# Moving the second stream's shifted inputs ahead of its low-rank products, and the first stream's v inputs and the whole second prelude behind the making of k's operands

## The chip, the core and the metric

The kernel runs on one core of one Trainium2 chip. TensorE (PE) multiplies matrices, with a sequencer of its own for weight loads (PEld); VectorE (DVE) and ScalarE (ACT) do elementwise work; GpSimd (POOL) does a few memsets; SyncE (SP) issues every DMA, one after the other, from one queue. Each engine has its own list of instructions; the trace shows the lists run in the order of the program, and an engine that waits at one instruction holds up the rest of its list. The metric is device microseconds of one execution.

## The reference

Two request groups ("streams" 0 and 1, 512 tokens by 1024 features each) pass through the same two layers. Layer 0 is an RWKV-7 time mixing with a forward and a backward scan, layer 1 a two-dimensional neighbourhood attention. The change touches the inputs of layer 0 only:

```
xn = rms_norm(x, pre_norm_g[0])
x_prev = jnp.pad(xn[:, :-1], ((0, 0), (1, 0), (0, 0)))
x_next = jnp.pad(xn[:, 1:], ((0, 0), (0, 1), (0, 0)))
xx = 0.5 * (x_prev + x_next) - xn
lerp = lambda j: xn + xx * mu[j]
r, k, v = heads(lerp(0) @ w_r), heads(lerp(1) @ w_k), heads(lerp(2) @ w_v)
z = xn @ w_z
for d in range(2):
    w_log = -softplus(-(w0[d] + tanh(lerp(3 + d) @ w1[d]) @ w2[d])) - 0.5
    a = sigmoid(a0[d] + (lerp(5 + d) @ a1[d]) @ a2[d])
    ...
```

`lerp(j)` is called a shifted input here; `lerp(3..6) @ w1, a1` are the low-rank products (1024 features to 4 times 64).

## The kernel before

Activations lie transposed: 128 features on the partitions and 512 tokens along the row, so a stream is 8 tiles of 128x512 (`k` = 0..7). Every fp32 product is split into a high and a low half of fp32r, and three products are made of one (hi·hi, hi·lo, lo·hi). A weight column (1024x128) comes in two DMAs `raw`; ACT casts each to `whi`, DVE subtracts to get `wlo` (four buffers of each). A column is 24 products of 128x512 on PE (lines 423 to 425 in the front, 802 to 804 in the scan stage). An operand pair (hi, lo) lies in two of 18 `act` buffers, nine pairs.

**The front** is all that comes before the scan stage. Its parts:

- prelude of stream 0: load x, norm (L434 to L465), `xn` (L525), `xx` (L532, L533), the low-rank weights (L479 to L487), the low-rank products (96 products, L549 to L551, into the banks `pf`, `pm`, `us`), their tail (L557 to L574), the shifted inputs for v (L581, 8 tiles, each saved to DRAM as `dlv`);
- eight columns z of stream 0, with its normalised x as operand;
- eight columns k of stream 0; the operands come from `shifted(0, 1)`: `xr` (L599) on DVE, cast on ACT, subtraction on DVE (L373 `act<-xr`). Each column's sums of squares go through L642, L646 and L649 to DRAM as `dss`. After the eighth they are loaded, rooted and inverted (L660, L662, L663) and stored as `drn`;
- prelude of stream 1: the same norm, `xn` and `xx`; then 8 pairs `ls` (ACT cast, DVE subtraction L373 `ls<-xn`) and the 96 low-rank products; the tail; then 24 shifted inputs for k, r and v (L581), each saved (`dlk`, `dlr`, `dlv`); `xn` is saved as `dlz`. All tiles `ls`, pairs and shifted inputs alike, share four buffers, taken in the order of the code;
- the operands of stream 0's r, `shifted(0, 0)`.

The tail of the low-rank products (L557 to L574) handles two pairs of results one after the other. For each pair: ACT copies `pf` (L562), DVE makes L563, L565, L570; then twice ACT L572 into the same 64 rows `u`, and a DMA saves them as `dhid`. There is one buffer `lm` and one buffer `lr`, and `u` is a part of `lr`: the second L572 waits until the first save has read `u`, and the second pair waits for the saves of the first.

**The scan stage** begins with columns r of stream 0 and the preparation of the first pair of heads: `rb` is loaded from `drn`, `k` from `dk`, `r` from `dr`; then L854 on DVE, L856 on ACT, L858 on DVE, the products L872 and L873 on PE, and from there the chain that feeds the scan's steps. Its order on PE, DVE and ACT is written by a planner that starts with all its clocks at zero, and so does not know when the front ends. L1622 are products without use that keep PE busy.

**The order in the front** is made by a scheduler that works through a simulated timeline: code that stands earlier has the higher priority, and an instruction is placed when its inputs are there in that simulated time. `run(g, (a, n))` advances generator `a` by `n` steps (yields) for each step of `g`; `both` joins two generators.

Of the kernel before, what the change touches and what calls it, by code (L numbers as in the profile page):

```python
# [14 lines left out]
ALU = mybir.AluOpType  # L15
# [214 lines left out]
class Trunk:  # L230
# [209 lines left out]
    def rstd(self, acc):  # L440
        run(self.rstds(acc))
        return acc
# [48 lines left out]
    def prelude(self, s):  # L491
        nc = self.nc
        vt, gps, act = nc.vector, nc.gpsimd, nc.scalar
# [3 lines left out]
        for k in range(KT):  # L497
            if s == 0 and k == self.WFIRST:
                self.first = [self.weight(self.a["w_z"][0])]
            t = self.t("xn", (P, T + 2), 16, F32, self.lp)  # L500
# [21 lines left out]
        xn, xx = [], []  # L522
        for k, t in enumerate(xs):
            x = t[:, 1:T + 1]
# [5 lines left out]
        for k, t in enumerate(xs):  # L530
# [3 lines left out]
            xx.append(u)  # L534
            yield
        self.shift[s] = xn, xx

        pm = self.p("pf", (P, 2, T))
        ps = (self.p("pm"), self.p("us"))
        for k in range(KT):  # L540
# [5 lines left out]
            for q2 in range(2):  # L546
                for out, w in ((pm[:, q2], self.wm), (ps[q2], self.wl)):
                    a, b = (m[:, k % 4] for m in w[2 * q2 + k // 4])
# [4 lines left out]
        for q2 in range(2):  # L553
# [21 lines left out]
                else:  # L575
                    self.save("hid", s, q, u)
            yield
        for kind, j in (("v", 2),) if s == 0 else (("k", 1), ("r", 0), ("v", 2)):
            for k in range(KT):
                t = self.t("ls", (P, T), 4, F32, self.lp)  # L580
                vt.scalar_tensor_tensor(t, xx[k], self.vec("mu", 8 * j + k), xn[k], op0=ALU.mult, op1=ALU.add)  # L581
                self.save("l" + kind, s, k, t)
                yield
        if s == 1:
# [550 lines left out]
    def step(self, q):  # L1135
# [59 lines left out]
        if both:  # L1195
            self.factors(q + 1, solved())
        else:
            run(solved())
# [513 lines left out]
    def run(self):  # L1712
        self.todo = [(s, pb) for s in range(2) for pb in range(4)]
        self.made, self.hid, self.shift = set(), {}, {}
        self.did = Counter()
        self.xz, self.os = [], [[], []]
        self.spare = None
        mid, prep, first = ExitStack(), ExitStack(), ExitStack()
        self.banks(mid, pf=1, pm=5 - self.SG - self.ZY, us=1)
        if self.SG:  # L1720
            self.banks(mid, pg=self.SG)
        self.zs = ExitStack()
        self.banks(self.zs, zy=self.ZY)
        self.gt = "zy"
        self.lp = self.pool(first, "right")
        a = self.prelude(0)
        for _ in range(self.FIRST):
            next(a)
        a = both(a, self.prelude(1))
        run(self.columns(0, "z", self.xz), (a, 1))  # L1730
        run(self.columns(0, "k", self.shifted(0, 1)), (a, 1))
        run(a)
        self.xr = self.shifted(0, 0)
        first.close()
        self.front = self.pool(mid, "right")
        self.pp = self.pool(prep, "right")
        self.AHEAD, self.AHEADW = self.SCAN_A, self.SCAN_W
        self.scan_phase(mid)
        self.rest(prep, mid)

    def rest(self, prep, mid):
# [15 lines left out]
        for p in range(self.NPA, NP):  # L1757
            run(self.inproj(0, self.xa, p), (a, self.POST0))
            queue.append(self.heads(0, p))
# [38 lines left out]
def both(*gs):  # L1798
    for g in gs:
        yield from g  # L1800
# [110 lines left out]
```

## Time and profile before

| | |
|---|---|
| median of three runs | 1686.07 us (1684.14 to 1687.42) |
| the profiled execution | 1683.88 us |
| its span, first to last instruction | 1682.1 us |
| what lies around the span | 1.8 us |
| PE busy / DVE busy / ACT busy | 1570.9 / 1227.8 / 984.0 us |
| mean granted TensorE clock | 0.971 |

The front takes roughly the first 190 us of the span: column z from 9 us, column k from 82 us, the last sum of squares of k at 170 us, the first instruction of the first pair of heads (L854) at 188.61 us. A row of the timeline gives the start in us, the duration in us, engine, line, operation, output and inputs, and in brackets the idle time of the engine just before and what ended it. A row of the windows gives for a stretch its length, then busy time and number of instructions of PE, PEld, DVE, ACT and POOL, the granted clock, the share of the DMA engines and GB/s. Busy times of successive instructions overlap a little, so a pace is read from one start to the next.

### The profile page before, as it was taken

What the parts mean: (1) busy time and instruction counts of PE and PEld (TensorE: products, weight loads), DVE (VectorE), ACT (ScalarE), POOL (GpSimd) and SP (SyncE); (2) the same over time, 40 slices, a digit from 0 to 9 for tenths busy, and PEclk for the clock granted to TensorE, in tenths of its full rate; (3) what the DMA queues carried; (4) which work ended last, traced back from release to release, by engine and by line L of the source; (5) the groups of instructions that cost most, each with busy time, mean ns of one, the idle gap of its engine ahead of it and who ended that gap; (6) DMA issues with size and microseconds to landing.
All of it is one profiled execution on the core that took longest, in us unless ns stands there. A gap on an engine that the chain in (4) does not pass through costs nothing.

```text
span 1682.1 us, 46291 instructions
## 1 busy us (share of the span) xinstructions
PE 1570.9 (93%) x18818; PEld 1201.2 (71%) x18818; DVE 1227.8 (73%) x2725; ACT 984.0 (58%) x1977; POOL 24.1 (1%) x94
## 2 busy tenths in 40 slices
PE   7989898899989998989998999999999899999998
PEld 6767666676766776767765767777777687777776
DVE  8985668688777697887888887865576856555564
ACT  5443655676655667755674665454577655555562
POOL 0000000000000000000000000000000000000000
PEclk9989999899999999999997999999999999999999
DMA  5435678678586786876776665554774347555553
GB/s 209 163 125 187 203 243 261 202 228 257 170 262 211 225 255 205 259 243 205 241 232 214 202 199 199 184 178 131 267 231 155 111 127 249 182 157 175 164 181 107
DMA packets 240821, 336.26 MB, mean 200 GB/s; under 512 B 53696, under 2 KB 119360, under 8 KB 240608
## 3 DMA queue, kind: packets, MB, share of 16 engines
q1 hardware_dynamic: 240608, 333.31, 61.6%
q8 instruction: 148, 2.42, 0.6%
q14 instruction: 65, 0.53, 0.1%
HBM read 227.71 MB, written 105.51 MB: 198 GB/s over the span
## 4 chain that ended last, share of the span: by engine, by line
PE 67%; DVE 11%; DMA 9%; ACT 8%; issue 4%; SPq 1%; DVEq 0%; POOL 0%; ACTq 0%; POOLq 0%
PE pm L802 7%; PE pg L423 6%; PE pg L424 6%; PE pg L425 6%; PE pm L804 5%; PE pm L803 5%; PE pf L1090 2%; PE sc L1433 2%; PE us L1209 2%; DMA cab<-dab 2%; PE po L1466 2%; PE pt L1451 2%; PE zy L1162 2%; PE us L1189 2%; PE zy L1213 1%
## 5 line engine op out<-in xcount | busy, mean ns | idle before, releaser
L802 PE MATMUL pm<-act,whi 128*128 128x512 f32 x640 | 287.6, 449 | 16.1 <-ACT act L771 7.2
L804 PE MATMUL pm<-act,wlo 128*128 128x512 f32 x640 | 256.7, 401 | 12.2 <-DVE wlo L723 12.2
L803 PE MATMUL pm<-act,whi 128*128 128x512 f32 x640 | 258.0, 403 | 5.1 <-DVE act L749 4.2
L423 PE MATMUL pg<-act,whi 128*128 128x512 f32 x448 | 182.4, 408 | 5.9 <-ACT act L372 5.5
L424 PE MATMUL pg<-act,whi 128*128 128x512 f32 x448 | 178.1, 398 | 0.1
L425 PE MATMUL pg<-act,wlo 128*128 128x512 f32 x448 | 177.5, 396 | 0.0
L802 PEld LDWEIGHTS pm<-act,whi 128*128 128x128 f32 x640 | 122.6, 192 | 63.8 <-issue 16.1
L372 ACT CAST whi<-raw 128x512 fp32r<-128x512 f32 x148 | 91.4, 619 | 129.3 <-PE pg L424 75.3
L804 PEld LDWEIGHTS pm<-act,wlo 128*128 128x128 f32 x640 | 123.4, 193 | 44.3 <-DVE wlo L723 16.9
L373 DVE TENSOR_TENSOR wlo<-raw,whi 128x512 fp32r<-128x512 f32 x148 | 101.4, 687 | 70.2 <-ACT whi L372 63.0
L803 PEld LDWEIGHTS pm<-act,whi 128*128 128x128 f32 x640 | 123.6, 193 | 29.6 <-DVE act L749 7.2
L723 DVE TENSOR_TENSOR wlo<-raw,whi 128x512 fp32r<-128x512 f32 x160 | 108.7, 684 | 42.9 <-ACT whi L721 39.5
L721 ACT CAST whi<-raw 128x512 fp32r<-128x512 f32 x160 | 98.1, 616 | 51.7 <-PE pm L803 14.5
L423 PEld LDWEIGHTS pg<-act,whi 128*128 128x128 f32 x448 | 84.8, 190 | 24.8 <-ACT act L372 6.1
L425 PEld LDWEIGHTS pg<-act,wlo 128*128 128x128 f32 x448 | 84.8, 189 | 17.9 <-issue 0.8
L424 PEld LDWEIGHTS pg<-act,whi 128*128 128x128 f32 x448 | 84.9, 190 | 17.4 <-issue 2.0
L996 DVE TENSOR_TENSOR N<-etmp,N 128x30 f32<-128x30 f32 (+14 forms) x240 | 78.5, 327 | 4.2
L994 DVE TENSOR_TENSOR etmp<-N 128x30 f32<-128x30 f32 (+14 forms) x240 | 78.3, 326 | 4.2
L1444 DVE CUSTOM_DVE_ANT_0 sb<-sc,bias 128x256 f32<-128x256 f32 x128 | 49.2, 419 | 31.1 <-PE pt L1451 23.5
L1090 PE MATMUL pf<-cab 64*64 64x128 f32 (+1 forms) x2048 | 67.9, 268 | 2.2 <-issue 2.1
L1447 ACT ACTIVATE sb<-sb,mx 128x256 f32<-128x256 f32 x128 | 63.9, 504 | 9.1 <-DVE mx L1446 9.0
L1113 DVE TENSOR_TENSOR AK<-zy,cc 128x256 f32<-128x256 f32 x63 | 26.6, 421 | 53.5 <-PE zy L1068 51.6
(389 smaller groups left out, 3389.7 us busy)
## 6 DMA issues: line engine op xcount, KB each, us to landing
dab<-ab SPq DMA_DIRECT2D x32, 1024.0 KB, 5.5
cab<-dab SPq DMA_DIRECT2D x64, 512.0 KB, 4.4
raw<-in_w_in_dram SPq DMA_DIRECT2D x128, 256.0 KB, 3.3
bias<-in_rpb_dram SPq DMA_DIRECT2D x32, 384.0 KB, 4.8
raw<-in_w_z_dram SPq DMA_DIRECT2D x32, 256.0 KB, 4.5
dz<-tmp SPq DMA_DIRECT2D x32, 256.0 KB, 3.0
raw<-in_w_k_dram SPq DMA_DIRECT2D x32, 256.0 KB, 4.0
dk<-tmp SPq DMA_DIRECT2D x32, 256.0 KB, 2.2
```

The lines of the kernel that those rows point to most:

```text
L372: self.nc.scalar.copy(hi, src)
L373: (eng or self.nc.vector).tensor_tensor(lo, src, hi.bitcast(F32), op=ALU.subtract)
L423: nc.tensor.matmul(ps, hi, x[k][0], start=(k == 0), stop=False)
L424: nc.tensor.matmul(ps, hi, x[k][1], start=False, stop=False)
L425: nc.tensor.matmul(ps, lo, x[k][0], start=False, stop=(k == KT - 1))
L721: nc.scalar.copy(hi, raw[h])
L723: nc.vector.tensor_tensor(lo, raw.pop(h), hi.bitcast(F32), op=ALU.subtract)
L802: nc.tensor.matmul(ps, hi[:, at], xh, start=(k == 0), stop=False)
L803: nc.tensor.matmul(ps, hi[:, at], xl, start=False, stop=False)
L804: nc.tensor.matmul(ps, lo[:, at], xh, start=False, stop=(k == KT - 1))
L996: vt.tensor_tensor(N[:, q + 1:, :q], tv, N[:, q + 1:, :q], op=ALU.add)
L1090: end = nc.tensor.matmul(st.f[half(a), h, 0, d, g] if st.last else st.f[half(a), h, :, d, g], ab[half(h), d, g, 2 * e[d] + 1 - a], rt if s ...
```

## The change

The 24 shifted inputs of stream 1 are made before its low-rank products instead of after them. The 8 shifted inputs for v of stream 0 leave its prelude and come after the whole prelude of stream 1. Prelude 0 is now run to its end before the code that makes the operands of k; prelude 1 starts after that code. The steps per column change from 1 to 0.6 (z) and 1.05 (k).

```diff
         self.shift[s] = xn, xx
+        if s == 1:
+            yield from self.shifts(1, (("k", 1), ("r", 0), ("v", 2)))
 
         pm = self.p("pf", (P, 2, T))
         ps = (self.p("pm"), self.p("us"))
...
-        for kind, j in (("v", 2),) if s == 0 else (("k", 1), ("r", 0), ("v", 2)):
+    def shifts(self, s, kinds):
+
+        xn, xx = self.shift[s]
+        for kind, j in kinds:
             for k in range(KT):
                 t = self.t("ls", (P, T), 4, F32, self.lp)
-                vt.scalar_tensor_tensor(t, xx[k], self.vec("mu", 8 * j + k), xn[k], op0=ALU.mult, op1=ALU.add)
+                self.nc.vector.scalar_tensor_tensor(t, xx[k], self.vec("mu", 8 * j + k), xn[k], op0=ALU.mult, op1=ALU.add)
                 self.save("l" + kind, s, k, t)
                 yield
...
         for _ in range(self.FIRST):
             next(a)
-        a = both(a, self.prelude(1))
-        run(self.columns(0, "z", self.xz), (a, 1))
-        run(self.columns(0, "k", self.shifted(0, 1)), (a, 1))
+        run(self.columns(0, "z", self.xz), (a, 0.6))
+        run(a)
+        x = self.shifted(0, 1)
+        a = both(self.prelude(1), self.shifts(0, (("v", 2),)))
+        run(self.columns(0, "k", x), (a, 1.05))
         run(a)
```

No instruction is added or removed on PE, DVE, POOL or in the DMA queue; ACT loads its function tables in other places. The orders of PE, DVE, ACT and SP differ up to the first pair of heads; behind it PE, DVE and ACT run in the same order as before. In the changed kernel line numbers are 2 higher from L537 to L580, 5 higher from there to the end of the front's functions, so L551 to L553 are before's L549 to L551, L586 is L581, L651 is L646, L567 and L572 are L565 and L570.

On PE, before, the low-rank products of stream 1 stand between the columns of k, the first of them (`ls`, `lw`) in k's second column; here around it:

```order
L425 MATMUL zy_1027<-act_939,wlo_1024 128x512
L646 MATMUL pm_1006<-tmp_1004,cc 2x512
L423 MATMUL zy_1027<-act_945,whi_1023 128x512
L424 MATMUL zy_1027<-act_944,whi_1023 128x512
L425 MATMUL zy_1027<-act_945,wlo_1024 128x512
L549 MATMUL pf_1049<-ls_1052,lw_303 128x512
L549 MATMUL pm_1050<-ls_1052,lw_292 128x512
L549 MATMUL us_1051<-ls_1052,lw_336 128x512
L423 MATMUL zy_1129<-act_903,whi_1121 128x512
```

Changed, the first of them stands behind the last product of the last column of k:

```order
L424 MATMUL zy_1481<-act_833,whi_1477 128x512
L425 MATMUL zy_1481<-act_834,wlo_1478 128x512
L551 MATMUL pf_1344<-ls_1347,lw_347 128x512
L551 MATMUL pm_1345<-ls_1347,lw_333 128x512
L551 MATMUL us_1346<-ls_1347,lw_383 128x512
L651 MATMUL pm_1454<-tmp_1452,cc 2x512
L552 MATMUL pf_1344<-ls_1348,lw_347 128x512
L553 MATMUL pf_1344<-ls_1347,lw_348 128x512
```

All 96 low-rank products of stream 1 have moved behind the 192 products of k; 13 products of the first r column lie among them, and the last two L646 (k's seventh and eighth sums of squares) stand behind the 3rd and the 24th of them.

On DVE, before, the eight subtractions `ls<-xn` are done when the first shifted input (L581) comes:

```order
L373 TENSOR_TENSOR ls_1187<-xn_765,ls_1186 128x512
L373 TENSOR_TENSOR ls_1220<-xn_767,ls_1219 128x512
L373 TENSOR_TENSOR ls_1255<-xn_769,ls_1254 128x512
L373 TENSOR_TENSOR wlo_1496<-raw_1491,whi_1495 128x512
L581 SCALAR_TENSOR_TENSOR ls_1327<-xx_976,cv,xn_755 128x512
L581 SCALAR_TENSOR_TENSOR ls_1347<-xx_982,cv,xn_757 128x512
```

Changed, the 24th shifted input stands ahead of the first subtraction, and the inverse of k's norms (before's L662 and L663) between the fourth and the fifth:

```order
L586 SCALAR_TENSOR_TENSOR ls_1303<-xx_1068,cv,xn_865 128x512
L586 SCALAR_TENSOR_TENSOR ls_1310<-xx_1085,cv,xn_867 128x512
L373 TENSOR_TENSOR ls_1348<-xn_853,ls_1347 128x512
L373 TENSOR_TENSOR ls_1383<-xn_855,ls_1382 128x512
L373 TENSOR_TENSOR ls_1405<-xn_857,ls_1404 128x512
L373 TENSOR_TENSOR ls_1427<-xn_859,ls_1426 128x512
L667 TENSOR_SCALAR tmp_1577<-tmp_1577 128x64
L668 RECIPROCAL tmp_1577<-tmp_1577 128x64
L373 TENSOR_TENSOR ls_1460<-xn_861,ls_1459 128x512
```

DVE comes to the low-rank pairs only after all 24 shifted inputs.

In SP's queue, before, the load of `rb` for the first pair of heads comes behind the last save `dhid`, and ahead of the output of the first r column (`dr`):

```order
L328 DMA raw_1797<-in_w_r_dram 128x512
L325 DMA dhid_300_1311<-lr_1297 64x512
L328 DMA raw_1838<-in_w_r_dram 128x512
L328 DMA rb_1788<-drn_411_1636 64x512 x2
L325 DMA dr_463_1780<-tmp_1778 128x512
L328 DMA k_1786<-dk_234_1002 128x512
```

Changed, all four saves and two outputs `dr` stand close ahead of it:

```order
L325 DMA dhid_390_1587<-lr_1558 64x512
L328 DMA tmp_1794<-in_lora_dram 128x512
L325 DMA dr_463_1780<-tmp_1778 128x512
L325 DMA dhid_391_1590<-lr_1558 64x512
L328 DMA raw_1863<-in_w_r_dram 128x512
L325 DMA dr_478_1826<-tmp_1824 128x512
L325 DMA dhid_394_1601<-lr_1593 64x512
L325 DMA dhid_395_1604<-lr_1593 64x512
L328 DMA rb_1788<-drn_389_1582 64x512 x2
L328 DMA k_1786<-dk_209_926 128x512
```

The loads for the first pair of heads have moved behind the fourth save of the tail and the second r column's output.

## The prediction

> **What bounds the kernel now.** I read the page first, then the windows over the front, then the timelines of PE, DVE, ACT and SP there.
>
> ```profile
> span 1682.1 us, 46291 instructions
> PE 1570.9 (93%) x18818; PEld 1201.2 (71%) x18818; DVE 1227.8 (73%) x2725; ACT 984.0 (58%) x1977; POOL 24.1 (1%) x94
> PE 67%; DVE 11%; DMA 9%; ACT 8%; issue 4%; SPq 1%; DVEq 0%; POOL 0%; ACTq 0%; POOLq 0%
> ```
>
> PE is the engine of the whole. Since behind the first pair of heads PE, DVE and ACT keep their order, and nothing there is tied to absolute time, I take it that the rest of the program moves as one piece with the moment at which that pair starts. So the question is when L854, L858 and L873 run.
>
> ```profile
> 20.00:82.00 62.00, 61.75 (x273) 50.35 (x273) 60.26 (x117) 27.71 (x48) 0.26 (x4) 1.00 0.41 141
> 82.00:104.00 22.00, 16.12 (x52) 11.30 (x51) 21.08 (x38) 13.01 (x21) 0.13 (x2) 0.69 0.31 114
> 104.00:138.00 34.00, 34.00 (x138) 24.09 (x137) 19.97 (x33) 11.55 (x20) 0.00 (x0) 1.00 0.30 105
> 138.00:167.00 29.00, 29.00 (x122) 21.80 (x121) 20.06 (x31) 11.89 (x22) 0.13 (x2) 1.00 0.70 238
> 167.00:192.00 25.00, 19.45 (x72) 13.27 (x70) 15.69 (x27) 12.92 (x25) 3.61 (x3) 0.93 0.72 239
> ```
>
> The windows show two engines taking turns. From 20 to 104 us DVE has work all the time (60.26 of 62, 21.08 of 22 us). From 82 to 104 us PE waits for it, loses its clock (0.69) and does 52 instructions where 62 us held 273, so 0.227 us each: 52 would have taken 11.8 us, 10.2 us are lost. From 104 to 167 us PE has no gap, and DVE is busy 40 of 63 us: k's columns and the low-rank products of stream 1 share PE, and DVE's 24 shifted inputs fall into the time that this leaves.
>
> ```profile
> 85.77 0.50 PE L424 MATMUL zy<-act,whi 128*128 128x512 f32 x1 [2.34 <-DVE act L373]
> 143.78 1.42 DVE L581 SCALAR_TENSOR_TENSOR ls<-xx,cv,xn 128x512 f32<-128x512 f32 x2 [2.21 <-PE us L550]
> 170.42 1.02 PE L646 MATMUL pm<-tmp,cc 128*2 128x512 f32 x2 [2.19 <-ACT tmp L642]
> 178.66 0.55 DVE L663 RECIPROCAL tmp<-tmp 128x64 f32<-128x64 f32 x1
> 188.61 0.75 DVE L854 SCALAR_TENSOR_TENSOR rb<-k,cv,rb 128x512 f32<-128x512 f32 x1 [2.03 <-DMA k<-dk]
> 191.23 0.69 DVE L858 TENSOR_TENSOR w2l<-tmp,w2h 128x512 fp32r<-128x512 f32 x1 [1.87 <-ACT w2h L856]
> 191.98 0.50 PE L873 MATMUL pm<-h,w2l 128*128 128x512 f32 x1 [0.22 <-DVE w2l L858]
> ```
>
> These are the marks: at 143.8 us the low-rank products of stream 1 give back `ls` buffers to the shifted inputs, and they end soon after, more than 20 us before the last sum of squares (170.42). Their tail then has time. L854 starts at 188.61, L858 at 191.23.
>
> **The change part by part.** No work goes away or comes new, so the sum is made of waits.
>
> *First term: when DVE reaches the first subtraction of a low-rank pair.* In the changed order DVE cannot pass the scaling of z's seventh column (L619) before PE has made that column. PE is unchanged up to the block of low-rank products of stream 0, from which z's third column now follows ten products earlier, at 42.65 - 10 x 0.227 = 40.4 us; from there to the end of the seventh column are 143 products, 32.5 us: 72.9 us.
>
> ```profile
> 42.65 0.40 PE L423 MATMUL zy<-act,whi 128*128 128x512 f32 x1
> 100.00 5.39 DVE L525 SCALAR_TENSOR_TENSOR xn<-xn,cv,acc 128x512 f32<-128x512 f32 x8 [0.80 <-ACT acc L465]
> 105.31 0.68 DVE L532 TENSOR_TENSOR xx<-xn 128x512 f32<-128x512 f32 x1
> 110.35 2.49 DVE L532 TENSOR_TENSOR xx<-xn 128x512 f32<-128x512 f32 x4
> 112.76 0.68 DVE L533 SCALAR_TENSOR_TENSOR xx<-xx,xn 128x512 f32<-128x512 f32 x1
> ```
>
> From that L619 to the first subtraction, 118 DVE instructions stand in the new order. 44 are of the form with a scale from `cv` (24 shifted inputs, 12 L599, 8 L525), 5.31 us for eight, 0.664 each: 29.2 us. The other 74 go at 2.41 us for four, 0.603 each: 44.6 us. So 72.9 + 73.8 = **146.7 us if DVE never waits**, against 143.8, when before all eight subtractions were already over. It will wait:
>
> ```profile
> L581 DVE SCALAR_TENSOR_TENSOR ls<-xx,cv,xn 128x512 f32<-128x512 f32 x32 | 23.0, 745 | 6.4 <-DMA dlr<-ls 2.7 <-PE us L550 2.2 <-DMA dlk<-ls 1.5
> ```
>
> The shifted inputs wait for their four buffers to be saved, 2.7 + 1.5 = 4.2 us before; I take the same. The norm of stream 1 goes PE, ACT, DVE, PE, ACT, DVE; 0.8 us stood before the L525 behind it, but in the new PE order nothing lies between L451 and L463, I take 3 us. The `act` pairs and weight halves are freed by PE's columns: 3 us, an estimate from the 2.34 us of such a wait above. With these 10.2 us the first subtraction comes at **157 us**; the bounds are 147 (no waits) and 163 (16 us of waits).
>
> PE meanwhile makes k's columns without the low-rank products between them. A column with its L646 costs 6.62 us:
>
> ```profile
> 160.60 1.02 PE L646 MATMUL pm<-tmp,cc 128*2 128x512 f32 x2
> 167.22 1.02 PE L646 MATMUL pm<-tmp,cc 128*2 128x512 f32 x2
> ```
>
> z's last column and the rest of stream 0's products end at 72.9 + 31 x 0.227 = 79.9, eight columns of k 53.0 us later, and some 7 us of waits for the operands and the norm bring it to 140 us. So PE stands still from 140 to 157 us: the 17 us are the price of the cover that is gone. What is won is most of the 10.2 us at 82 to 104 us, and it is lost again at this place.
>
> *Second term: the low-rank products.* 96 products at 0.230 us (12 of them from 141.05 to 143.81) are 22.1 us; 13 products of r 3.0; the two L646 0.95 each, 1.9; six L1622 1.3. The inverse of the norms now stands between the fourth and the fifth subtraction, behind 24 products: its way from L646 to the end of L663 was 8.8 us (170.42 to 179.21), the work of PE in that time 7.5 us: 1.3 us more. PE starts cold after the gap:
>
> ```profile
> 97.81 0.77 PE L423 MATMUL zy<-act,whi 128*128 128x512 f32 x1
> 101.37 0.55 PE L425 MATMUL zy<-act,wlo 128*128 128x512 f32 x1
> 141.05 0.39 PE L549 MATMUL pf<-ls,lw 128*128 128x512 f32 x1
> 143.81 0.40 PE L424 MATMUL zy<-act,whi 128*128 128x512 f32 x1
> ```
>
> In such a stretch 8 products took 3.56 us instead of 1.8: 1.7 us. Sum 31 us; the first product needs only the cast, which comes with the subtraction: end at **188 us** (bounds 147 + 28 = 175 and 163 + 34 = 197).
>
> *Third term: the tail, which lies bare.* Each half of `u` is saved before the next is written:
>
> ```profile
> 156.59 0.61 ACT L572 ACTIVATE lr<-lr 64x512 f32<-64x512 f32 x1
> 157.51 0.53 SPq L325 DMA_DIRECT2D dhid<-lr  x1
> 161.95 0.63 ACT L572 ACTIVATE lr<-lr 64x512 f32<-64x512 f32 x1 [3.52 <-DMA dhid<-lr]
> 162.61 0.47 SPq L325 DMA_DIRECT2D dhid<-lr  x1
> 176.21 0.46 SPq L325 DMA_DIRECT2D dhid<-lr  x1
> 181.01 0.45 SPq L325 DMA_DIRECT2D dhid<-lr  x1
> 182.19 1.11 SPq L328 DMA_DIRECT2D rb<-drn  x2
> 185.61 0.42 SPq L328 DMA_DIRECT2D k<-dk  x1
> ```
>
> From the last product to the first L572: L562, L563, L565, L570 at 0.6 each, and DVE stands between them behind stream 0's v inputs and an operand of v that has to be written and read back through DRAM: 6 us, an estimate (bounds 3 and 10). L572 0.6 and its save's issue 0.1. First save to second 5.1 (157.51 to 162.61). Second save to the second pair 4.4 (157.51 to 161.95), three DVE instructions 1.9, L572 0.7, third save to fourth 4.8. Then `rb` 0.5 after it, `k` 1.2 after that, and 3.0 from the issue of `k` to L854 (185.61 to 188.61). Sum 28.3 us by these rows; before, that round trip ran while the queue moved 238 GB/s, and here less moves. Other saves landed sooner:
>
> ```profile
> dk<-tmp SPq DMA_DIRECT2D x32, 256.0 KB, 2.2
> ```
>
> Between 2.2 and 4.4 us I take 3.3, so 1.1 us off each of the three, 3.3 in all: 25 us. L854 then runs at 213 us, 24.4 later; L858 follows 0.75 later instead of 2.6, at 213.8: **22.6 us later** than 191.23. PE reaches the end of the second r column (36 products, 8 us after the low-rank ones, and the wait for r's weight halves behind the same DVE rows) near 202 us, so it waits too.
>
> On the length of a save, the Trainium skill, "DMA: Bandwidth & Descriptors", section "Anatomy of one DMA — SWDGE (gpsimd) path", states for transfers issued from GpSimd a fixed cost of about 2.0 us and the bytes at 436 GB/s on top. By it a save of 128 KB would be back after an estimated 2.3 us, the three round trips would take 6.3 us less than the first rows give, and the sum would be 19.6 us. The trace has 4.4 us from issue to the released ACT in a loaded stretch, so it does not bear the page's figure out there.
>
> The profiled execution took 1683.9 us and lies 2.2 us under the median of its runs, so the sum gives 1706.5 for such an execution and 1708.7 against the median; I give **1709 us**. Its own range: all low bounds together, 175 us and 18.5 of tail (3 us to L572, 2.2 for each save), put L858 3 us later; all high ones, 197 and 32, put it 39 later. They will hardly come together: +11 to +33 us, 1697 to 1719.
>
> **The rivals.** *The front gets shorter, the other side.* DVE has no waits and the new order takes away the loss at 82 to 104 us. If the first subtraction came by 133 us, the products would end by 133 + 24 (no cold start, no norm between) = 157, a tail of 18.5 us would bring `rb` and `k` at 176, and only the norms would gate them, which end earlier too; L854 could be 6 us earlier: 1680 us. For it: PE does lose 10.2 us there. Against it: 133 is 14 us under the sum without waits (146.7), and DVE was full from 20 to 104 us. 4%; a tie with before, in which the waits and gains cancel, 3%.
>
> *The tail is hidden.* If the saves came back fast and DVE were not held up between L562 and L570, the start would be set by PE: the second r column ends at 188 + 8 = 196 instead of 189.9. That is 6 us: 1692 us. For it: the four saves are small. Against it: L854 and L858 stand on DVE behind the last L570, and `rb` on SP behind the fourth save. 13%.
>
> *It costs more.* The v inputs of stream 0 are written at the very end and read back for the second group of the scan stage; DVE is held at the operand L749 while r's weight halves (L723) wait behind it, and PE goes cold a second and third time. With 10 us for the way to L572 and full 28 us of saves, L858 comes 33 us or more later: 1719 us and above. 13%.
>
> **How the numbers follow.** My forecast has 67%. Range 1694 to 1722: it takes in most of the hidden tail's upper half and the lower half of the costlier case. Slower by over 0.2% (3.4 us, about what three runs of this kernel can tell from no change, as their own spread is 3.3 us) are the forecast, the hidden tail and the costlier case: 93%; within 0.2% 3%; faster 4%.
>
> **What would show it.** Right: PE idle for 10 us or more before the first L551 on `ls` (DVE or ACT named as what ended it); the 24 L586 finished between 150 and 160 us; four `dhid` saves near 195 to 210 us with ACT L577 waiting for them; L859 at about 213 us waiting for `k<-dk`; from there on every row about 23 us late; and the 82 to 104 us loss mostly gone. Wrong: low-rank products starting before 147 us, L859 before 195 us, or a difference that grows or shrinks by more than a few us behind the first pair of heads.

## The result and the profile after

| | before | changed |
|---|---|---|
| median beside each other on one chip | 1685.11 us (1682.66 to 1687.42, 4 runs) | 1710.55 us (1708.97 to 1717.89, 4 runs) |
| ratio, 95% interval | | 1.0167 (1.0140 to 1.0194) |
| profiled execution / its span | 1683.88 / 1682.1 us | 1708.97 / 1707.2 us |
| first `w2l` of the first pair of heads (L858, now L863) | 191.23 us | 217.28 us |

Slower by 25 us; 1709 was predicted. The totals on the page of the changed kernel:

```profile
span 1707.2 us, 46296 instructions
PE 1573.1 (92%) x18818; PEld 1203.9 (71%) x18818; DVE 1228.5 (72%) x2725; ACT 983.0 (58%) x1975; POOL 24.2 (1%) x94
```

The busy times are those of before to 2.2 us, so the 25 us are nearly all waiting. Where they stand is shown by PE's waits, summed by line (us in total, times, longest), and by the windows of the changed kernel (same columns as before):

```profile
PE pf L551 <- ACT ls L372: 16.3, 1, 16.3
PE pm L877 <- ACT w2h L861: 8.0, 2, 7.6
```

```profile
20.00:82.00 62.00, 61.96 (x274) 50.45 (x273) 52.26 (x103) 24.65 (x42) 0.13 (x2) 1.00 0.34 112
82.00:104.00 22.00, 18.18 (x75) 13.51 (x73) 19.77 (x33) 14.16 (x25) 0.13 (x2) 0.91 0.31 102
104.00:138.00 34.00, 33.54 (x124) 22.47 (x125) 27.80 (x47) 16.47 (x30) 0.13 (x2) 0.91 0.54 185
138.00:167.00 29.00, 12.74 (x44) 7.66 (x42) 20.72 (x32) 7.66 (x14) 0.00 (x0) 0.71 0.57 206
167.00:192.00 25.00, 22.35 (x97) 17.95 (x96) 8.34 (x14) 4.12 (x8) 0.00 (x0) 1.00 0.14 42
192.00:220.00 28.00, 15.13 (x46) 11.08 (x47) 9.94 (x17) 11.24 (x21) 3.73 (x5) 0.69 0.58 190
```

DVE has 14 instructions less between 20 and 82 us (103 for 117), and PE made 75 instructions for 52 from 82 to 104 us: a win of 23 x 0.227 = 5 us. It is paid back between 138 and 167 us, where PE made 44 instead of 122, and behind 192 us. The timeline of the changed kernel there, for PE, DVE, ACT and SP:

```profile
157.78 0.80 PE L551 MATMUL pf<-ls,lw 128*128 128x512 f32 x1 [16.26 <-ACT ls L372]
192.97 0.79 PE L807 MATMUL pm<-act,whi 128*128 128x512 f32 x1 [3.62 <-ACT whi L726]
213.16 0.80 PE L877 MATMUL pm<-h,w2h 128*128 128x512 f32 x1 [7.64 <-ACT w2h L861]
```

```profile
152.77 4.33 DVE L586 SCALAR_TENSOR_TENSOR ls<-xx,cv,xn 128x512 f32<-128x512 f32 x6 [0.33 <-DMA dlr<-ls]
157.75 0.69 DVE L373 TENSOR_TENSOR ls<-xn,ls 128x512 fp32r<-128x512 f32 x1 [0.66 <-ACT ls L372]
205.61 0.69 DVE L565 TENSOR_TENSOR lr<-lm 128x512 f32<-128x512 f32 x1 [4.72 <-DMA dhid<-lr]
216.62 0.75 DVE L859 SCALAR_TENSOR_TENSOR rb<-k,cv,rb 128x512 f32<-128x512 f32 x1 [8.59 <-DMA k<-dk]
217.28 0.68 DVE L863 TENSOR_TENSOR w2l<-tmp,w2h 128x512 fp32r<-128x512 f32 x1
```

```profile
188.99 0.59 ACT L564 COPY lm<-pf 128x512 f32<-128x512 f32 x1 [6.08 <-PE pf L553]
191.78 0.62 ACT L752 CAST act<-xr 128x512 fp32r<-128x512 f32 x1 [2.21 <-DMA xr<-dlv]
...
196.89 0.63 ACT L574 ACTIVATE lr<-lr 64x512 f32<-64x512 f32 x1 [2.15 <-DVE lr L572]
...
202.55 0.63 ACT L574 ACTIVATE lr<-lr 64x512 f32<-64x512 f32 x1 [2.39 <-DMA dhid<-lr]
...
207.84 0.63 ACT L574 ACTIVATE lr<-lr 64x512 f32<-64x512 f32 x1 [2.56 <-DVE lr L572]
210.81 0.63 ACT L574 ACTIVATE lr<-lr 64x512 f32<-64x512 f32 x1 [2.34 <-DMA dhid<-lr]
```

```profile
197.54 0.54 SPq L325 DMA_DIRECT2D dhid<-lr  x1
203.21 0.46 SPq L325 DMA_DIRECT2D dhid<-lr  x1
208.49 3.42 SPq L325 DMA_DIRECT2D dhid<-lr  x2
212.00 1.19 SPq L328 DMA_DIRECT2D rb<-drn  x2
213.24 0.58 SPq L328 DMA_DIRECT2D k<-dk  x1
```

Read in order of time: PE has made all columns of k and stands 16.26 us, because DVE comes to the first `ls<-xn` only behind the 24th shifted input (that one ends at 157.1). The low-rank products then last to 189 us (ACT L564 waits for the last of them). Behind them PE has only r's columns; the four saves `dhid` go one after the other, `rb` and `k` stand behind them in SP's queue, and L859 waits for `k`.

### The profile page after: what moved, and what is told of

It reads as the page before. It is cut to its first block, busy times and chain, and to the rows that moved or that the text cites. A ratio compares the mean times of both kernels' runs of the same rounds, so it can differ in the third digit from the quotient of the medians.

```text
span 1707.2 us, 46296 instructions
## 1 busy us (share of the span) xinstructions
PE 1573.1 (92%) x18818; PEld 1203.9 (71%) x18818; DVE 1228.5 (72%) x2725; ACT 983.0 (58%) x1975; POOL 24.2 (1%) x94
## 4 chain that ended last, share of the span: by engine, by line
PE 65%; DVE 12%; DMA 10%; ACT 9%; issue 3%; SPq 0%; DVEq 0%; POOL 0%; ACTq 0%; POOLq 0%
PE pm L807 7%; PE pg L423 5%; PE pg L424 5%; PE pg L425 5%; PE pm L809 5%; PE pm L808 5%; PE pf L1095 2%; PE sc L1438 2%; PE us L1214 2%; PE zy L423 2%; PE zy L1167 2%; PE zy L424 2%; PE zy L425 2%; PE us L1194 2%; PE po L1471 2%
## 5 line engine op out<-in xcount | busy, mean ns | idle before, releaser
L807 PE MATMUL pm<-act,whi 128*128 128x512 f32 x640 | 289.2, 452 | 15.2 <-ACT act L776 5.7
L807 PEld LDWEIGHTS pm<-act,whi 128*128 128x128 f32 x640 | 123.9, 194 | 63.0 <-issue 15.9
L1118 DVE TENSOR_TENSOR AK<-zy,cc 128x256 f32<-128x256 f32 x63 | 26.6, 422 | 55.3 <-PE zy L1073 53.8
```

The source lines that it names most:

```text
L807: nc.tensor.matmul(ps, hi[:, at], xh, start=(k == 0), stop=False)
```

## The experiments

Twelve kernels ran. The table gives for each the start of the first `w2l`, how much later that is than the 191.23 us before, how much longer its profiled execution was than the 1683.88 us before, and the ratio of its times to the kernel before on the same chip.

| run | first `w2l` | later by | execution longer by | ratio (95%) |
|---|---|---|---|---|
| changed | 217.28 | 26.1 | 25.1 | 1.0167 (1.0140 to 1.0194) |
| e1: shifted inputs behind | 205.85 | 14.6 | 15.7 | 1.0084 (1.0056 to 1.0111) |
| e2: shifted inputs ahead, alone | 204.37 | 13.1 | 11.0 | 1.0070 (1.0046 to 1.0094) |
| e3: v inputs in place | 216.50 | 25.3 | 26.6 | 1.0146 (1.0116 to 1.0175) |
| e4: buffers apart | 202.47 | 11.2 | 10.9 | 1.0096 (1.0060 to 1.0133) |
| e5: two places for `u` | 211.19 | 20.0 | 24.3 | 1.0120 (1.0071 to 1.0169) |
| e6: paces 1 and 1 | 214.26 | 23.0 | 24.0 | 1.0140 (1.0100 to 1.0180) |
| e7: four places | 208.17 | 16.9 | 15.5 | 1.0102 (1.0071 to 1.0133) |
| e8: late second prelude alone | 199.25 | 8.0 | 8.7 | 1.0036 (1.0013 to 1.0058) |
| e9: the same, 2 steps | 196.12 | 4.9 | 8.2 | 1.0022 (1.0002 to 1.0042) |
| e10: v inputs early, 2 steps | 203.15 | 11.9 | 20.0 | 1.0098 (1.0064 to 1.0131) |
| e11: v inputs early | 205.36 | 14.1 | 14.4 | 1.0075 (1.0044 to 1.0107) |
| e12: buffers apart and four places | 201.63 | 10.4 | 7.8 | 1.0063 (1.0040 to 1.0086) |

The two columns of delays agree within 4.3 us in all rows but e10. So in all these orders but that one, most of the time is decided by where the first pair of heads starts. Single executions of the kernel before on these chips lay between 1676 and 1696 us, so differences of a few us between rows are read from the timelines, not from the times. A timeline is one execution too: up to the end of the low-rank products the lists of PE, DVE, ACT and SP in e5 are those of the changed kernel, yet e5 got there 2.5 us sooner (ACT L564 at 186.44 against 188.99). Differences under some 3 us between two rows of the table show nothing.

**e1: the shifted inputs of stream 1 behind its products again.**

```diff
         self.shift[s] = xn, xx
-        if s == 1:
-            yield from self.shifts(1, (("k", 1), ("r", 0), ("v", 2)))
...
                     self.save("hid", s, q, u)
             yield
+        if s == 1:
+            yield from self.shifts(1, (("k", 1), ("r", 0), ("v", 2)))
```

> The changed kernel with one part undone: the 24 shifted inputs of stream 1 stand behind its low-rank products again; the first stream's v inputs, the late second prelude and the steps of 0.6 and 1.05 stay. By the theory (the shifted inputs ahead of the pairs are what costs): no idle time of 10 us on PE before the first low-rank product of stream 1; these products lie between the columns of k and end by 175 us; 17 shifted inputs and the last two saves dhid now stand on DVE and SP behind the inverse of the norms, so the first L859 comes some 0 to 8 us later than the 188.6 us of before, and the time is 1688 us (1682 to 1698). By the rival that the late second prelude or the v inputs at the end are what costs: over 1700 us, L859 behind 205 us.

Half right. The 16 us wait is gone, but the time, 1700.72 us, lies above the range, and the rival (over 1700 us, L859 behind 205 us) came close: the counterpart of L859 ran at 203.14 us. The timeline of e1, PE and ACT:

```profile
163.51 1.02 PE L652 MATMUL pm<-tmp,cc 128*2 128x512 f32 x2 [1.32 <-ACT tmp L648]
193.15 0.80 PE L808 MATMUL pm<-act,whi 128*128 128x512 f32 x1 [23.08 <-ACT whi L727]
```

```profile
191.95 0.62 ACT L753 CAST act<-xr 128x512 fp32r<-128x512 f32 x1 [6.07 <-DMA xr<-dlv]
```

PE comes to the last sum of squares of k, with the low-rank products done, at 163.5 us, 7 us sooner than before. It then has a few products of r and the products without use left, and from 170 us on it has nothing for 23 us: r's weight halves stand on ACT behind the cast of an operand of v that has to be read back from `dlv`, which DVE wrote last of all, behind the 24 shifted inputs. That is the second of the changed places.

**e2: the shifted inputs ahead, and nothing else of the change** (the diff of e1 the other way round, in the kernel before; the saves of `xn` as `dlz` stay behind).

> Before, with one part of the change alone: the 24 shifted inputs of stream 1 ahead of its low-rank products; v inputs, second prelude and steps as before. By the theory: the loss at 82 to 104 us stays; DVE is at the first subtraction ls<-xn at about 146 us, since 59 rows stand between the end of the norm at 105 us and it, some 37 us, and some 4 us of waits for saves; PE makes the columns of k without cover and stands still for 5 to 12 us; products end near 177 us, the tail of about 28 us lies bare as in the changed kernel, L859's counterpart runs near 204 us: 1698 us (1690 to 1706), so about half of the whole loss. By the rival that the order of the shifted inputs doesn't matter: 1685 us. By a third, in which this part alone makes the whole loss and what the changed kernel won at 82 to 104 us was nothing: 1710 us or more.

As the theory had it: 1698.30 us, the first `w2l` 13.1 us late. e2's windows and PE's timeline:

```profile
82.00:104.00 22.00, 16.81 (x50) 11.91 (x49) 21.07 (x37) 12.12 (x19) 0.13 (x2) 0.61 0.32 111
```

```profile
147.53 0.79 PE L556 MATMUL pf<-ls,lw 128*128 128x512 f32 x1 [9.87 <-ACT ls L372]
```

The wait for the first subtraction is 9.87 us here, and the loss at 82 to 104 us stays (50 products). So the order of the shifted inputs costs by itself about half, and it does not bring the win.

**e5 and e7: the saves of the tail.** e5 puts the halves of `u` in different rows, e7 (not shown) also gives the second pair its own place in `lm`, so that no row waits for a save.

```diff
             for q in (2 * q2, 2 * q2 + 1):
+                if s == 1:
+                    u = lr[64 * (q % 2):64 * (q % 2) + 64, T:2 * T]
                 act.activation(u, y[64 * (q % 2):64 * (q % 2) + 64], AF.Tanh if q < 2 else AF.Copy)
```

> The changed kernel, with the two halves of u in different rows of the buffer lr, so that the second L574 doesn't wait for the save of the first; the second pair still waits for the saves of the first pair. PE keeps its order. By the theory (the saves, one after the other, set the start of the first pair of heads): the first two saves dhid are under 1.5 us apart instead of 5.7, the last two too instead of 3.0; the second pair still waits some 4 us for the buffer; L859 comes at about 211 us instead of 216.6; 1705 us (1702 to 1708). By the rival that PE sets the start (second column of r, end at 204.5 us): no more than 1 us sooner, 1709.5 to 1711.

> The changed kernel, with each of the four results in a place of its own (two in the buffer lr, two in the unused part of lm, which grows by 2 columns), so that no row of the tail waits for a save. By the theory: the four saves dhid are issued between 196 and 203 us, rb and k right behind them, L859 at about 206 us instead of 216.6; the second column of r on PE ends at 204.5 us as before, so that now PE and DVE are nearly even, and the first product on w2h starts at 207 us: 9 to 10 us off, 1701 us (1698 to 1704). By the rival that PE sets the start: 1710 us. By the rival that the saves were the whole loss: 1690 us or less.

SP's timeline of e5, then of e7:

```profile
195.10 1.17 SPq L325 DMA_DIRECT2D dhid<-lr  x2
203.81 1.10 SPq L325 DMA_DIRECT2D dhid<-lr  x2
205.63 1.11 SPq L328 DMA_DIRECT2D rb<-drn  x2
```

```profile
195.57 1.18 SPq L325 DMA_DIRECT2D dhid<-lr  x2
200.09 1.09 SPq L325 DMA_DIRECT2D dhid<-lm  x2
201.28 1.21 SPq L328 DMA_DIRECT2D rb<-drn  x2
```

L859's counterpart came at 210.52 in e5 (211 expected) and at 207.50 in e7 (206 expected), against 216.62. A part of that is not the saves' doing, because both executions ended the low-rank products sooner, ahead of the rows that were edited. ACT's first row of the tail, in e5 and then in e7, against 188.99 in the changed kernel:

```profile
186.44 0.59 ACT L564 COPY lm<-pf 128x512 f32<-128x512 f32 x1 [6.08 <-PE pf L553]
```

```profile
186.81 0.59 ACT L565 COPY lm<-pf 128x512 f32<-128x512 f32 x1 [6.08 <-PE pf L553]
```

From that row to L859 the tail took 27.6 us in the changed kernel, 24.1 in e5 and 20.7 in e7: 3.6 and 6.9 us belong to the saves. PE has the same order of products in all three, but for one sum of squares of k. So the saves set the start of the scan stage, and the rival in which PE sets it falls: with the waits for the saves gone the same PE work starts 7 us sooner. The times follow only roughly, and both lie above their ranges: 1705.44 us for e7, whose interval of the ratio lies below that of the changed kernel, and 1708.94 us for e5, whose interval overlaps with it.

**e3: the v inputs back in the first prelude.**

```diff
+        if s == 0:
+            yield from self.shifts(0, (("v", 2),))
...
-        a = both(self.prelude(1), self.shifts(0, (("v", 2),)))
+        a = self.prelude(1)
```

> The changed kernel, with the first stream's v inputs back at the end of its own prelude; shifted inputs of stream 1 ahead of the pairs, late second prelude and steps as in the changed kernel. By the theory that the shifted inputs ahead of the pairs set the end of the low-rank products, and their bare tail the rest: PE still stands still for 12 us or more before the first low-rank product of stream 1; in the tail DVE no longer makes v inputs and the operand read back from them, so the first save dhid comes some 3 us sooner than 197.5; 1707 us (1702 to 1712). By the rival that the v inputs at the end are the main loss (in the run with the shifted inputs behind, PE waited 23 us for r's weights behind ACT's cast of an operand read back from dlv): 1695 us or less.

1711.12 us; in the range, but not by the way that was told. PE's wait for the first product grew to 18.02 us and ended at 161.65 us (66 products at 82 to 104 us instead of 75), the first save went out at 199.28 us and not sooner. What the tail won was lost ahead of it: made early, the eight inputs hold up DVE in the front by about as much (161.65 for 157.78). The rival, that they are the main loss, falls: here they are back in place, and the loss is what it was.

**e4: two buffers for the shifted inputs, two for the pairs.**

```diff
-                hi, lo = (self.t("ls", (P, T), 4, F32R, self.lp) for _ in range(2))
+                hi, lo = (self.t("lq", (P, T), 2, F32R, self.lp) for _ in range(2))
...
-                t = self.t("ls", (P, T), 4, F32, self.lp)
+                t = self.t("ls", (P, T), 2, F32, self.lp)
```

> The changed kernel, with the four shared buffers ls cut in two and two: two for the shifted inputs, two (lq) for the low-rank pairs. The pairs then don't take turns with the shifted inputs: the eight subtractions stand on DVE between them, the first ahead of all, the last behind the 22nd; on PE 60 of the 96 products lie in the first column of r. By the theory that the wait for the 24 shifted inputs is what makes PE stand still: no idle time of 10 us on PE before the first low-rank product, the products end near 175 instead of 189 us, L859 near 202 us, 1695 us (1688 to 1706); the shifted inputs themselves get slower, since each waits for the save two before. By the rival that DVE's work and not the shared buffers sets the end: within 3 us of 1710.

The wait of PE is gone. e4's window and the last low-rank product:

```profile
138.00:167.00 29.00, 25.99 (x98) 18.29 (x97) 20.41 (x32) 7.33 (x13) 0.00 (x0) 0.94 0.42 155
```

```profile
175.28 0.39 PE L553 MATMUL us<-lq,lw 128*128 128x512 f32 x1
```

The products end at 175.7 instead of 189 us, the first `w2l` comes 14.8 us sooner than in the changed kernel. The amount of DVE work is the same, but its order is not: the first subtraction now stands ahead of all 24 shifted inputs, 40 us sooner than the 157.75 of the changed kernel.

```profile
117.23 0.69 DVE L373 TENSOR_TENSOR lq<-xn,lq 128x512 fp32r<-128x512 f32 x1
```

So e4 shows that the order on DVE makes the wait. The buffers are taken in the order of the code, so sharing them makes the scheduler write that order; at run time the shifted inputs of the changed kernel waited only 1.4 us for them ahead of the first subtraction (1.02 for `dlk`, 0.33 for `dlr`). The median, 1704.66 us, is above the profiled execution's 1694.79, and the ratio says a smaller win (1.0096) than the timeline.

**e8 and e9: the late second prelude alone.** The kernel before, with

```diff
-        a = both(a, self.prelude(1))
-        run(self.columns(0, "z", self.xz), (a, 1))
-        run(self.columns(0, "k", self.shifted(0, 1)), (a, 1))
+        run(self.columns(0, "z", self.xz), (a, 0.6))
+        run(a)
+        x = self.shifted(0, 1)
+        a = self.prelude(1)
+        run(self.columns(0, "k", x), (a, 1.05))
```

and 2 in place of 1.05 in e9.

> Before, with one part of the change alone: the first prelude run to its end ahead of the code for k's operands, the second one started behind it, steps of 0.6 and 1.05; v inputs and the shifted inputs of stream 1 stand as before. It differs from the run with the shifted inputs behind only by the place of the v inputs. By the theory: the loss at 82 to 104 us is half gone as in the changed kernel (about 75 products instead of 52), the last sum of squares of k comes some 5 us sooner than 170.4, and with the v inputs in place PE makes r's columns right behind it, not after 23 us; six shifted inputs and the last saves dhid stand behind the inverse of the norms, so L854 comes at about 186 us: 1683 us (1679 to 1691). By the rival that the late second prelude itself made the loss of that run: 1698 to 1702 us.

> As the run before it, with 2 steps instead of 1.05 in the columns of k, so that the second prelude goes faster: all shifted inputs and the whole tail of the low-rank products stand on DVE ahead of the inverse of the norms, as they do before the change. By the theory both good things come together: half of the loss at 82 to 104 us is won, nothing lies bare, L854 at about 183 us, 5 to 6 us off: 1680 us (1676 to 1686), the fastest of all. By the rival that what is won at 82 to 104 us is lost again before the first pair of heads whatever the order: 1685 us, no difference.

Both missed, theory and rival: 1693.39 us (1693.09 without the one of its ten executions that took 2129.91) and 1692.02 us. e8 made 62 products at 82 to 104 us, so the win is smaller with the v inputs in place, and the last save `dhid` (191.91 us) stood behind its shifted inputs. In e9 there is no win at all; its window, and PE's row L451 (a sum of the norm of stream 1) in e9 and then in e8:

```profile
82.00:104.00 22.00, 11.51 (x50) 9.10 (x48) 19.79 (x32) 12.33 (x22) 0.13 (x2) 0.84 0.23 76
102.12 1.84 PE L451 MATMUL pm<-ones,acc 128*128 128x1 f32 x8 [9.10 <-DVE acc L438]
```

```profile
105.73 0.95 PE L451 MATMUL pm<-ones,acc 128*128 128x1 f32 x8
```

DVE's list is the same in e8 and e9 up to the last L438 (101.64 and 101.28 us), and between 20 and 104 us DVE ran 147 and 146 rows, against 154 before. What differs is PE's list. With 2 steps L451 stands ahead of the second column of k, 24 products, and PE stands at it for 9.10 us until DVE has added up `acc`; in e8 it stands behind that column and doesn't wait. The last sum of squares then comes at 173.28 us in e9, later than the 170.42 of before. So taking DVE work out of 20 to 104 us isn't enough for the win: PE's list must also have something else to do ahead of the row that waits for DVE. And the work that was taken out needs a place before 170 us, or it lies bare.

**e11 and e10: e1 with the v inputs ahead of the 24 shifted inputs;** e10 with 2 steps too.

```diff
         if s == 1:
+            yield from self.shifts(0, (("v", 2),))
             yield from self.shifts(1, (("k", 1), ("r", 0), ("v", 2)))
```

> The run with the shifted inputs behind (e1), with one thing moved: the first stream's v inputs stand behind the low-rank tail of the second prelude but ahead of the 24 shifted inputs, not behind them. By the theory that in e1 PE's 23.1 us without work came from ACT's cast of an operand read back from the last-written dlv, with r's weight halves queued behind it: that wait is under 8 us here, L859's counterpart comes at 192 us (188 to 197) instead of 203.1; the shifted inputs of stream 1 still stand in part behind the inverse of the norms: 1690 us (1685 to 1696). By the rival that the number of shifted inputs behind the inverse, whichever they are, makes e1's loss: 1698 us or more.

> As the run before it, with 2 steps instead of 1.05 in the columns of k: the low-rank products are done in the sixth column of k, and only eight shifted inputs stand behind the inverse of the norms. The first stream's v inputs are out of the stretch up to 104 us, where DVE is the bound. By the theory: 75 or more products at 82 to 104 us (52 before), last sum of squares of k at 165 us instead of 170.4, inverse of the norms at 174, the first w2l at 186 to 188 us instead of 191.2: 1682 us against 1686 (1677 to 1688). By the rival that DVE's eight shifted inputs and their saves behind the inverse hold up the first pair of heads by as much as was won: 1686 to 1692 us.

Both were tries for a kernel that beats the one before, and both failed: 1695.20 us, just inside e11's range, and 1702.13 us, above both ranges of e10. In e11 the 23 us of e1 did go from r's columns (first product at 174.62 us after 3.04 us of idle time), but L861 came at 204.69 us, where 192 was expected. SP's timeline of e11:

```profile
192.37 0.51 SPq L325 DMA_DIRECT2D dlr<-ls  x1
193.64 5.73 SPq L325 DMA_DIRECT2D dlv<-ls  x8
199.46 1.12 SPq L328 DMA_DIRECT2D rb<-drn  x2
```

The load of `rb` stands in the queue behind the saves of the last shifted inputs, whichever stream they are for. So e11's rival had the mechanism of the end right, though not PE's wait, and its time (1698 us or more) was not reached. In e10 56 products were made at 82 to 104 us (75 expected); as in e9, PE stood at L451, for 8.00 us. And e10's execution is 8 us longer still than its first `w2l` says: by the same DVE rows it is 11.9 us behind the kernel before at the first `w2l`, 15.3 at `kp<-kp,th` (325.31 us before, 340.62 in e10) and 20.8 at `etmp<-N` (760.52 and 781.36). Why it grows is not explained.

**e6: the steps per column back at 1 and 1.**

```diff
-        run(self.columns(0, "z", self.xz), (a, 0.6))
+        run(self.columns(0, "z", self.xz), (a, 1))
...
-        run(self.columns(0, "k", x), (a, 1.05))
+        run(self.columns(0, "k", x), (a, 1))
```

> The changed kernel with the steps per column back at 1 and 1 instead of 0.6 and 1.05; everything else of the change stays. By the theory that the place of the shifted inputs sets the wait and not the paces: PE stands still for 12 us or more before the first low-rank product of stream 1, L859 between 212 and 221 us, 1710 us (1705 to 1715). By the rival that the paces make a good part of the loss: 1700 us or less.

1706.95 us, 13.60 us of wait ahead of the first product (152.71), L859 at 213.59: the first `w2l` comes 3 us sooner than in the changed kernel, no more than two executions of the same order differ by. So the paces aren't shown to matter here; that they don't make the loss is.

**e12: both cures at once,** the buffers of e4 and the places of e7.

> The changed kernel with both cures at once: two buffers for the shifted inputs and two for the pairs, and a place of its own for each of the four results of the tail. By the theory that the loss is the sum of the two (products late behind 24 shifted inputs; saves of the bare tail one after the other): with the buffers alone the first w2l came at 202.5 us, with the four places alone it came 9 us sooner than in the changed kernel (208.2 against 217.3); together 193.5 us (190 to 198), 2 us behind the 191.2 of before, 1690 us (1685 to 1697). By the rival that behind the products PE's columns of r set the start and the places bring nothing more: 202 us and 1697 us or more.

They don't add up: 1695.81 us lies inside the range, but the first `w2l` came at 201.63, not at 193.5, and only 0.8 us sooner than with the buffers alone. DVE and SP of e12:

```profile
189.89 0.75 DVE L589 SCALAR_TENSOR_TENSOR ls<-xx,cv,xn 128x512 f32<-128x512 f32 x1 [3.53 <-DMA dlv<-ls]
```

```profile
166.25 10.21 SPq L325 DMA_DIRECT2D dlv<-ls  x8
185.72 1.40 SPq L325 DMA_DIRECT2D dhid<-lr  x2
187.21 3.79 SPq L325 DMA_DIRECT2D dlv<-ls  x2
193.94 1.11 SPq L325 DMA_DIRECT2D dhid<-lm  x2
195.76 1.11 SPq L328 DMA_DIRECT2D rb<-drn  x2
```

The four results wait for no save now, but a v input between them does: with two buffers each shifted input waits for the save two before (eight saves take 10.21 us), and it holds the rows of the tail behind it on DVE. The rival's 202 us is what came, and it was right in part: PE was through with r's second column only at about 195 us (1.55 us of idle time before its first product on w2h at 196.90), so 193.5 was out of reach. But from there PE waited 4.96 us more for `w2l`, so the tail still sets the start.

## Why the prediction was right

**First subtraction.** Predicted at 157 us as 146.7 without waits and 10.2 us of waits, with PE idle for 17 us; it ran at 157.75 with 16.26. That the shifted inputs ahead make this wait is shown by e1 (gone when they go back), by e2 (9.87 us when they alone come forward) and by e4 (gone when the first subtraction stands ahead of them). The count of DVE's rows carried this sum. Its waits came to about the predicted total, 9 us, but not from the places named: the saves of the four buffers cost 1.4 us instead of 4.2, and the largest wait is one that the sum doesn't have, for ACT in the tail of the first prelude:

```profile
DVE h L597 <- ACT h L596: 4.5, 3, 2.5
```

And e5 came to its first subtraction at 154.35 us by the same lists. So that the moment was right to 1 us is in part luck; that PE would stand still behind 24 shifted inputs is not.

**The win at 82 to 104 us.** Predicted as mostly of 10.2 us; it was half, 5 us (75 products for 52). It did not enter the sum by itself, so the sum stands. With neither part moved there is none (e2, 50 products); with the late second prelude alone it is small (e8 and e3, 62 and 66); with the v inputs out of the way too it is 75 to 83 (changed, e5). No run moved the v inputs alone. In e9 and e10 (50 and 56) it is lost again at L451.

**Products.** Predicted 31 us, to 188; they took from 157.78 to 189.35, 31.6 us. Small terms were off both ways: 12 products of r lie among them, not 13, the products without use took 2.3 us instead of 1.3, and PE did not stand still for the norms (1.3 us).

**Tail.** This term was too small: 25 us predicted up to L859, 27.6 measured (188.99 to 216.62); with the 1 us by which the products ended later it makes the 3.5 us between the 213.8 predicted for the first `w2l` and the 217.28 measured. By its pieces, in us:

| piece | predicted | measured |
|---|---|---|
| last product to first save | 6.7 | 8.55 |
| first save to second | 4.0 | 5.67 |
| second to third | 5.9 | 5.28 |
| third to fourth (L574 at 207.84 to L574 at 210.81) | 3.7 | 2.97 |
| fourth save to `rb` and `k` | 1.7 | 1.8 |
| `k` to L859 | 3.0 | 3.4 |

So the way to the first save was mis-sized, and of the 1.1 us taken off each round trip the first did not come; the sum by the rows of before alone, 28.3 us, would have been nearer. That the saves are a real part of this term, and PE's columns don't set the start, is shown by e5 and e7 (3.6 and 6.9 us off the tail).

**One piece.** Predicted 1:1 behind the first pair of heads: 26.1 us there, 25.1 us in the execution (1708.97 us, 1706.5 by the sum). At the end this holds, on the way it doesn't. By the same DVE rows the changed kernel is 31.1 us late at `kp<-kp,th` (325.31 us before, 356.36 changed) and 22.5 us late at `tmp<-pg,vs` (1437.45 and 1459.93). The prediction had called a difference that grows or shrinks by more than a few us a sign of being wrong; here it does both, by 5 and 8.6 us, and that the two nearly cancel by the end is luck. What makes it stays open. Over the twelve other orders the two columns of the table differ by 0.3 to 4.3 us, and by 8 us in e10.

**The rivals.** The hidden tail falls: L859 waited for the `k` behind the four saves, and e5 and e7 show that it moves with them. The shorter front: part of the gain is there, but only 5 us. Costs more: PE did wait 3.62 us for r's halves at L807, behind the operand read back from `dlv`, but the saves lay over it.

**What the prediction did not part.** It put the DVE rows ahead of the first subtraction into one sum, whichever edit brought them there. Measured at the first `w2l`, each from one execution and so to some 3 us, the shifted inputs ahead cost 13.1 us alone (e2) and 11.4 us on top of the rest (changed less e1); the late second prelude with its paces costs 8.0 us alone (e8); the v inputs at the end cost 6.6 us where the shifted inputs stand behind (e1 less e8) and 0.8 us where they stand ahead (changed less e3), where they take from the front what they spare the tail.

What stays open: why the difference grows and shrinks behind the first pair of heads, in e10 above all, and whether any order wins the 10 us at 82 to 104 us without paying later; none of these did.

## What to carry to other kernels

Work that an idle-looking engine does beside a busy one is covered only until the busy one runs out: put first what leads to the next stage (here the pairs and the tail of the low-rank products), and leave what is only stored for later (shifted inputs) to any stretch that still has cover. Where two kinds of tiles share buffers and a queue, look at the order in both: the short chain takes its turn behind the long one on the engine, in the buffers, and again in the queue of saves. Look at the place of a waiting row in its own engine's list, too: in e9 one early row held up PE for 9 us, with 24 products behind it that e8 makes ahead of it. And before curing a wait, ask what stands next behind it; in e1, e11 and e12 the cure of one wait brought out the next.

## What the runs showed of the hardware

- The long wait shows in PE's clock too: from 138 to 167 us 0.71 was granted, and the first product behind the gap took 0.80 us, against 0.39 for the last one of e4; from 167 to 192 us it is back at 1.00. The prediction had 1.7 us for it, and the products' 31 us hold with it.
- The granted clock was not the same in two executions of the same order: 0.91 from 82 to 104 and from 104 to 138 us in the changed kernel, 1.00 in both stretches in e5, whose lists are the same there; e5 made 83 products in the first of them instead of 75. Whether the clock made the difference or followed from it is not shown.
- The same small save gave its buffer back after very different times within 10 us: 5.0 us from the first save's issue (197.54) to the ACT row that waited for it (202.55), 2.4 us from the second (203.21) to DVE L565 (205.61). Between the first pair SP also issued a load (`tmp<-in_lora_dram`, 1.29 us) and a save. In e3, where that load isn't issued there, the first save's buffer came back after 2.4 us (199.28 to 201.67). So a price of a save taken from one row held here to a factor of two. The Trainium skill, "DMA: Bandwidth & Descriptors", section "Anatomy of one DMA — SWDGE (gpsimd) path", whose figures are for transfers issued from GpSimd and from which the prediction worked out an estimate of 2.3 us, agrees with the later trips (2.4 us) and not with the first (5.0 us).
